# Head norms' root by bit operations on VectorE, projections placed behind the score matmuls, and the second page's request ahead of three low halves

## Chip, core and metric

The kernel runs on one core of one Trainium2 chip. The metric is the device time of one launch in microseconds (us), as the median of the runs; lower is better.

## What is computed

One layer of a decoder for a prompt of 1024 tokens and 32 sample tokens (8 sequences of 4). One input projection feeds two groups of heads: sparse attention (8 query heads, 2 key and value heads) over the keys that an indexer picks, and retention (8 heads) with a norm over each head. Both are gated, concatenated and projected out. Cut to what the change touches:

```python
def _index_select(qi, wi, ki, qpos, kpos, topk):
    s = jnp.einsum('bqhd,bsd->bqhs', qi, ki) * (D_IDX ** -0.5)
    score = jnp.einsum('bqh,bqhs->bqs', wi, jax.nn.relu(s))
    ...
    top_val, top_idx = lax.top_k(score, topk)      # 256 of the prompt's 1024; sample: of 8192 paged keys
...
def _head_norm(o):
    mu = jnp.mean(o, axis=-1, keepdims=True)
    var = jnp.mean(jnp.square(o - mu), axis=-1, keepdims=True)
    return (o - mu) * lax.rsqrt(var + EPS)
```

The outputs are y for prompt and sample, the new keys, values and indexer keys, and the retention's states.

## The kernel before

Tile's scheduler sets the order of each engine's instructions when the kernel is built; each engine then runs its list in that order. The program calls below say what belongs together, and the lists say what runs when. PE is TensorE, DVE VectorE, ACT ScalarE, POOL GpSimd and SP the queue that issues most transfers.

**Weights** (`load_w`, L176 on): a block of 256 columns is loaded as two halves of 512 rows on SP; ACT casts each half to the high part (`whi`, L196), and POOL subtracts to get the low part (`wlo`, L197) in eight pieces, one for each 128 rows. `wraw`, `whi` and `wlo` have two buffers each. A projection unit (`proj_b`, L277 to L279) is one block of 128 columns for one of three groups of tokens (384, 416 or 256), with 8 x 3 = 24 matmuls (high x high, low x high, high x low) into `pb`.

**Scores, up to some 166 us.** `index_scores` (L530 on) handles the query blocks qb 2 to 7 of 128 rows. For each of 8 indexer heads PE multiplies into one of two PSUM pairs `si` (L383, L384; (qb+1) x 128 columns), ACT takes the relu (L542, two buffers `r`) and DVE adds the weighted result to `score` (L543); at a block's end POOL masks the diagonal (L545). Between the heads, `unit(rate)` adds the rate to a counter and issues a projection unit of the generator `units` at each whole number: 12 units of qa (results copied to `qst` by ACT and DVE, L364, L365), 6 of keys and values (`kava`), 12 of the gate (`ga`). The rate is 0.3 in the blocks 5 to 7.

**Pages, up to some 297 us.** Sixteen pages of the sample's indexer keys follow (loop over b and a, L868 on). `key_pages` (L421) issues one indirect DMA from POOL's queue into a `slab`. The two slabs share the tag `big` with the two query tiles of the scores, so page 0's waits for the last matmul on `qis0`, page 1's for the last on `qis1`, and later ones for the `pox` matmuls of the page two before. DVE transposes each half (L875), PE multiplies (`pox`, L877), ACT takes a relu (`rl`, L880) and PE sums the heads (`py`). Between them go steps of the prompt's bisection for the 256th score (DVE, ACT; L700 to L733) and projection units, 2.5 a page at first, then 2.0 and 1.25.

**Retention, some 297 to 604 us.** Four pairs of heads hp 0 to 3. For each, `pqk` and `pvg` projections, rope on DVE (`rp`, L1116 to L1118), the chunked retention on PE (`ret`, `second`, masked by DVE as `sm`, L1148), and for hp 0 to 2 `norm_gate` (L1151 on), once for 128 rows x 16 and once for 32 rows x 2 numbers: statistics by DVE, `gv` = variance + eps (L1163), Sqrt on ACT (L1166, with a table load), reciprocal and one Newton step on DVE (L1167 to L1182), the scaling on ACT and DVE (L1186, L1188), the gate on POOL (L1191). The last pair's factors come from `last_factors` (L1200 on), which has the same root (L1209 to L1214). The selection of the sample's keys (`sel`, `cx`, `eq`) runs beside it on DVE. Attention follows (`sa`, L1743), then the output projection and the last gate.

## Time and profile before

| | |
|---|---|
| median of 3 runs | 1011.24 us (1006.64 to 1012.78) |
| profiled execution, own time | 1009.07 us |
| its span | 1007.0 us |
| mean granted clock of TensorE | 0.969 |
| busy: PE, DVE, ACT, POOL | 945.4, 664.2, 453.5, 338.8 us |

A row of a timeline reads: start, duration, engine, line, operation, out<-in, shapes, count, and in brackets the idle time ahead with what ended it. A row of windows gives for a stretch the busy time and count of each engine, the granted clock, the share of the DMA engines and GB/s. A row of waits reads: engine and line that waited, what it waited for, the total in us, how often, the longest.

### The profile page before, as it was taken

The page shows a single profiled execution, that of the slowest core. Times are in us where ns is not written, and L with a number is a line of the kernel's source. Part 1 is how long each engine was busy: PE and PEld are TensorE (multiplying, and loading weights), DVE is VectorE, ACT ScalarE, POOL GpSimd, SP SyncE. Part 2 cuts the span into 40 slices and gives each one's busy share as a digit, 9 for nine tenths or more (in the row PEclk, how much of TensorE's full clock was granted, in tenths as well). Part 3 has the DMA queues.
Part 4 walks back from the last instruction along what each step waited for, and adds up shares of the span by engine and source line. Part 5 has one row for each costly group of instructions (what it writes and reads, how often), then busy time and mean ns, then how long its engine had stood idle before and what let it go on. Part 6 is the DMA issues. An engine that isn't in the chain of part 4 may idle for free.

```text
span 1007.0 us, 18956 instructions
## 1 busy us (share of the span) xinstructions
PE 945.4 (94%) x6983; PEld 798.3 (79%) x6983; DVE 664.2 (66%) x1936; ACT 453.5 (45%) x1005; POOL 338.8 (34%) x444
## 2 busy tenths in 40 slices
PE   4999995989999999998899988999999999999998
PEld 3989993557678988988898866566567999999998
DVE  6747667879946669889679558777754323953332
ACT  5645555345324877224422537465554434432210
POOL 4205215112406326247325226454323322233300
PEclk8999998899999999999899968999999999999999
DMA  8323234567534112032013554533221312422211
GB/s 277 100 73 102 100 111 119 188 206 255 182 104 102 41 43 69 20 91 67 24 43 102 135 162 138 163 105 97 63 79 55 112 53 84 143 86 90 86 39 37
DMA packets 102127, 104.36 MB, mean 104 GB/s; under 512 B 22002, under 2 KB 92210, under 8 KB 99602
## 3 DMA queue, kind: packets, MB, share of 16 engines
q1 hardware_dynamic: 96274, 76.93, 25.8%
q0 software_dynamic: 5760, 26.22, 8.4%
q8 instruction: 55, 0.90, 0.4%
q14 instruction: 38, 0.31, 0.1%
HBM read 80.36 MB, written 22.76 MB: 102 GB/s over the span
## 4 chain that ended last, share of the span: by engine, by line
PE 63%; DVE 14%; DMA 9%; issue 8%; POOL 3%; ACT 2%; SPq 1%; DVEq 0%; POOLq 0%; ACTq 0%
PE pb L277 5%; PE pb L278 4%; PE pb L279 4%; PE ob L1772 3%; PE ptp L1764 3%; PE pg L287 3%; PE pg L289 3%; PE pg L288 3%; PE po L287 3%; PE po L288 3%; PE po L289 3%; PE pox L877 2%; DMA kx<-in_cache_kidx,kidx 2%; PE pvg L287 2%; PE pvg L288 2%
## 5 line engine op out<-in xcount | busy, mean ns | idle before, releaser
L1277 POOL DMA_INDIRECT kvs<-in_cache_kv,idx x64 | 64.2, 1004 | 59.0 <-ACT pT L1769 32.0
L287 PE MATMUL pvg<-whi_vgb,xh 128*128 128x256 f32 x256 | 77.0, 301 | 2.5 <-DVE rp L1118 2.5
L288 PE MATMUL pvg<-wlo_vgb,xh 128*128 128x256 f32 x256 | 75.8, 296 | 0.8 <-POOL wlo_vgb L197 0.8
L287 PE MATMUL pqk<-whi_qkb,xh 128*128 128x256 f32 x256 | 73.8, 288 | 1.5 <-DVE rp L1118 1.2
L289 PE MATMUL pvg<-whi_vgb,xl 128*128 128x256 f32 x256 | 74.6, 292 | 0.0
L287 PE MATMUL po<-whi_o,yTh 128*128 128x256 f32 x256 | 73.3, 286 | 0.4 <-DVE yaT L1783 0.4
L288 PE MATMUL pqk<-wlo_qkb,xh 128*128 128x256 f32 x256 | 73.3, 287 | 0.0
L289 PE MATMUL pqk<-whi_qkb,xl 128*128 128x256 f32 x256 | 73.1, 285 | 0.0
L288 PE MATMUL po<-wlo_o,yTh 128*128 128x256 f32 x256 | 72.9, 285 | 0.0
L287 PE MATMUL pg<-whi_g,yTh 128*128 128x256 f32 x256 | 72.7, 284 | 0.0
L289 PE MATMUL po<-whi_o,yTl 128*128 128x256 f32 x256 | 72.6, 284 | 0.0
L289 PE MATMUL pg<-whi_g,yTl 128*128 128x256 f32 x256 | 72.3, 282 | 0.0
L288 PE MATMUL pg<-wlo_g,yTh 128*128 128x256 f32 x256 | 72.2, 282 | 0.0
L197 POOL TENSOR_TENSOR wlo_g<-wraw_g,whi_g 128x256 fp32r<-128x256 f32 x32 | 27.1, 881 | 88.0 <-ACT whi_g L196 87.9
L1961 DVE TENSOR_TENSOR sgm<-pu,sgm 128x256 f32<-128x256 f32 x32 | 13.6, 424 | 64.5 <-PE pu L289 61.2
L1753 ACT ACTIVATE L<-L,mn 128x128 f32<-128x128 f32 (+7 forms) x64 | 49.6, 777 | 14.5 <-DVE mn L1749 14.1
L543 DVE SCALAR_TENSOR_TENSOR score<-r,wi,score 128x384 f32<-128x384 f32 (+5 forms) x42 | 42.6, 1015 | 20.2 <-ACT r L542 18.2
L287 PEld LDWEIGHTS pvg<-whi_vgb,xh 128*128 128x128 f32 x256 | 50.0, 195 | 4.6 <-issue 2.1
L288 PEld LDWEIGHTS pvg<-wlo_vgb,xh 128*128 128x128 f32 x256 | 50.0, 195 | 1.3 <-POOL wlo_vgb L197 1.0
L287 PEld LDWEIGHTS pqk<-whi_qkb,xh 128*128 128x128 f32 x256 | 48.3, 188 | 3.1 <-issue 2.4
L287 PEld LDWEIGHTS po<-whi_o,yTh 128*128 128x128 f32 x256 | 49.0, 191 | 2.2 <-issue 1.6
L289 PEld LDWEIGHTS pvg<-whi_vgb,xl 128*128 128x128 f32 x256 | 50.1, 196 | 0.3
(559 smaller groups left out, 3115.9 us busy)
## 6 DMA issues: line engine op xcount, KB each, us to landing
wraw_qkb<-in_w_in SPq DMA_DIRECT2D x16, 256.0 KB
wraw_vgb<-in_w_in SPq DMA_DIRECT2D x16, 256.0 KB
wraw_o<-in_w_out SPq DMA_DIRECT2D x8, 512.0 KB
qas<-qas_d SPq DMA_DIRECT2D x8, 512.0 KB
xr<-in_x_prompt SPq DMA_DIRECT2D x8, 512.0 KB
wraw_g<-in_w_ple_gate SPq DMA_DIRECT2D x8, 512.0 KB
out_y_prompt<-sgm SPq DMA_DIRECT2D x32, 128.0 KB
qas_d<-qst SPq DMA_DIRECT2D x8, 384.0 KB
```

Of the source, the lines that this page charges most:

```text
L197: nc.gpsimd.tensor_tensor(lo[:, k, :n], raw, hi[:, k, :n].bitcast(F32), op=ALU.subtract)
L277: nc.tensor.matmul(pt[:m, :n], wh, xh[:, k, ts], start=(k == 0), stop=False)
L278: nc.tensor.matmul(pt[:m, :n], wh, xl[:, k, ts], start=False, stop=False)
L279: nc.tensor.matmul(pt[:m, :n], wl, xh[:, k, ts], start=False, stop=(k == KC - 1))
L287: nc.tensor.matmul(pt[:, :n], ah, hi[:, k, :n], start=(k == 0), stop=False)
L288: nc.tensor.matmul(pt[:, :n], ah, lo[:, k, :n], start=False, stop=False)
L289: nc.tensor.matmul(pt[:, :n], al, hi[:, k, :n], start=False, stop=(k == kc - 1))
L543: nc.vector.scalar_tensor_tensor(sc, r[:, :n], wi[:, qb, h:h + 1], sc if h else place[:, :n], op0=ALU.mult, op1=ALU.add)
L1277: return nc.gpsimd.indirect_dma_start(out=dst, out_offset=None, in_=kvflat, in_offset=bass.IndirectOffsetOnAxis(ap=idx, axis=0))
L1753: behind[0] = nc.scalar.activation(L[:, :n], L[:, :n], AF.Exp, bias=least, scale=-1.0, accum_out=sm[:, i4:i4 + 1])
L1764: nc.tensor.transpose(tp[:, i4 * 128:i4 * 128 + 128], P[i4][:, kb * 128:kb * 128 + 128], ident)
L1772: nc.tensor.matmul(ob[64 * o:64 * o + 64, :256], vtok[:, kb, kv * 64:kv * 64 + 64], pT[:, o * 256:o * 256 + 256], start=(kb == 0), stop=(k ...
```

## The change

1. `inverse_root(y, z, v)`: eleven DVE operations (a shift, a subtraction from a constant on the bits, three Newton steps of three operations) in place of Sqrt, reciprocal and one Newton step, in `norm_gate` and in `last_factors`.
2. In the blocks 5 to 7, `between` counts 0.375 for each head instead of 0.3 and its units may be issued only behind a score matmul: the first three calls behind the last one of block 2, later ones behind the score matmul issued last. The units of the page loop stand behind the last score of all, at 2, 2.5, 2 and 2 for the first four pages and 12.5/12 after.
3. The low halves of `kava` are left at five; the other three are issued behind the request of page 1, which is now made ahead of the page loop.

```diff
@@ -173,7 +173,7 @@
 
     last_w = [None]
 
-    def load_w(name, pieces, lazy=False):
+    def load_w(name, pieces, lazy=False, late=0):
 
 
         n = sum(p[1] for p in pieces)
@@ -199,7 +199,12 @@
 
         if lazy:
             return hi, lo, raws, convert()
-        for _ in convert():
+        todo = convert()
+        for _ in range(KC - late):
+            next(todo)
+        if late:
+            return hi, lo, raws, todo
+        for _ in todo:
             pass
         return hi, lo, raws
 
@@ -377,11 +382,13 @@
             a = slice(o * 64, o * 64 + 64)
             nc.vector.tensor_tensor(kl[a, gs], s, kh[r0:r0 + 64, gs].bitcast(F32), op=ALU.subtract)
 
+    scored = [None, None]
+
     def mm_qk(pt, st, kh, kl, n):
         for c in range(0, n, 512):
             w = min(512, n - c)
             nc.tensor.matmul(pt[:, c:c + w], st, kh[:, c:c + w], start=True, stop=False)
-            nc.tensor.matmul(pt[:, c:c + w], st, kl[:, c:c + w], start=False, stop=True)
+            scored[1] = nc.tensor.matmul(pt[:, c:c + w], st, kl[:, c:c + w], start=False, stop=True).ins
 
     scp = ExitStack()
     sp_ = scp.enter_context(pool("scp"))
@@ -414,13 +421,15 @@
     def slab(name):
         return big.tile([128, 8, 384], F32R, tag="big", bufs=2, name=name)
 
+    paged = [None]
+
     def key_pages(i):
 
         b, a = i // 2, i % 2
         kx = slab("kx").bitcast(F32).rearrange("p a b -> p (a b)")
-        nc.gpsimd.indirect_dma_start(
+        paged[0] = nc.gpsimd.indirect_dma_start(
             out=kx[:, :2048], out_offset=None, in_=pages,
-            in_offset=bass.IndirectOffsetOnAxis(ap=kidx[:, a * 8 + b:a * 8 + b + 1], axis=0))
+            in_offset=bass.IndirectOffsetOnAxis(ap=kidx[:, a * 8 + b:a * 8 + b + 1], axis=0)).ins
         return kx
 
     def use_qa(j, g, pt):
@@ -487,7 +496,7 @@
                 proj_b(w, c0, 128, use, (g,))
                 yield
 
-        w = [load_w("qa0", wcols((QA, 256))), load_w("qa1", wcols((QA + 256, 256)))]
+        w.extend([load_w("qa0", wcols((QA, 256))), load_w("qa1", wcols((QA + 256, 256)))])
         loads = [("kava", KA), ("ga0", GA), ("ga1", GA + 256), None]
         for i in range(5):
             for a in range(2):
@@ -496,8 +505,9 @@
                        (lambda g, pt: use_ga(2 * i - 6 + a, g, pt)))
                 yield from triple(w[i], a * 128, use)
             if i < 3:
-                w.append(load_w(loads[i][0], wcols((loads[i][1], 256))))
-
+                w.append(load_w(loads[i][0], wcols((loads[i][1], 256)), late=0 if i else 3))
+
+    w = []
     unit_gen = units()
     tick = [0.0]
 
@@ -643,6 +653,7 @@
             nc.vector.tensor_scalar(place[:, i * 256:i * 256 + 256], C("slots"), i * 256.0, -1.0e-36,
                                     op0=ALU.add, op1=ALU.mult)
         index_scores(2, qiss[0])
+        scored[0] = scored[1]
         for qb in (3, 4):
             index_scores(qb, qiss[0], more)
         for _ in last:
@@ -651,8 +662,15 @@
         nc.sync.dma_start(O["kidx_sample"].rearrange("o b t d -> (o b t) d"), ktok[:NS, 8, :64])
         unit(0)
         kx0 = key_pages(0)
+        nth = [0]
+
+        def between():
+            nth[0] += 1
+            with tc.issue_after(scored[nth[0] > 3]):
+                unit(0.375)
+
         for qb in (5, 6, 7):
-            index_scores(qb, qiss[1], lambda: unit(0.3))
+            index_scores(qb, qiss[1], between)
 
     bss_ = ExitStack()
     bs = bss_.enter_context(pool("bs", side="right"))
@@ -865,10 +883,14 @@
         if pend:
             pend.pop(0)()
 
+    kxs = [kx0, key_pages(1)]
+    with tc.issue_after(paged[0]):
+        for _ in w[2][3]:
+            pass
     for b in range(8):
         rls = []
         for a in range(2):
-            kx = key_pages(2 * b + a) if b or a else kx0
+            kx = key_pages(2 * b + a) if b else kxs[a]
             po = pair("pox")
             for up in range(2):
                 kT = kx[:, 2048:] if up == 0 else sx.tile([128, 1024], F32, tag="kT", bufs=1, name="kT")
@@ -884,7 +906,8 @@
             while tickb[0] >= 1:
                 tickb[0] -= 1
                 step(bp)
-            unit(2.5 if 2 * b + a < 2 else 2.0 if 2 * b + a < 4 else 1.25)
+            with tc.issue_after(scored[1]):
+                unit((2, 2.5, 2, 2)[2 * b + a] if b < 2 else 12.5 / 12)
         pend.append(lambda b=b, rls=rls: head_sum(b, rls))
     while pend:
         later()
@@ -1148,6 +1171,16 @@
             nc.vector.tensor_tensor(sm[:rows, j, :rows], sc, mask_ap, op=ALU.mult)
         return r, qkT, sm
 
+    def inverse_root(y, z, v):
+
+        V = nc.vector
+        V.tensor_scalar(y.bitcast(I32), v.bitcast(I32), 1, None, op0=ALU.logical_shift_right)
+        V.tensor_scalar(y.bitcast(I32), y.bitcast(I32), -1.0, float(0x5F3759DF), op0=ALU.mult, op1=ALU.add)
+        for _ in range(3):
+            V.scalar_tensor_tensor(z, y, -0.5, y, op0=ALU.mult, op1=ALU.mult)
+            V.tensor_tensor(z, z, v, op=ALU.mult)
+            V.scalar_tensor_tensor(y, z, 1.5, y, op0=ALU.add, op1=ALU.mult)
+
     def norm_gate(acc, sgs, ntb, rows, tb0, hp):
 
         nh = ntb * 2
@@ -1163,23 +1196,8 @@
         nc.vector.tensor_tensor(v_.rearrange("p (t h) -> p t h", h=2),
                                 mv[:rows, :nh, 1].rearrange("p (t h) -> p t h", h=2),
                                 epsn[:rows, tb0:tb0 + ntb, 2 * hp:2 * hp + 2], op=ALU.add)
-        nc.scalar.activation(y_, v_, AF.Sqrt)
-        nc.vector.reciprocal(y_, y_)
-        one = [slice(i, i + 1) for i in range(nh)]
-        if nh == 2:
-            for i in one:
-                nc.vector.tensor_scalar(z_[:, i], y_[:, i], y_[:, i], v_[:, i], op0=ALU.mult, op1=ALU.mult)
-        else:
-            nc.vector.tensor_tensor(z_, y_, y_, op=ALU.mult)
-            nc.vector.tensor_tensor(z_, z_, v_, op=ALU.mult)
-        nc.vector.tensor_scalar(z_, z_, -0.5, 1.5, op0=ALU.mult, op1=ALU.add)
-        if nh == 2:
-            for n, i in enumerate(one):
-                nc.vector.tensor_scalar(y_[:, i], y_[:, i], z_[:, i], None, op0=ALU.mult)
-                nc.vector.tensor_scalar(z_[:, i], mv[:rows, n, 0:1], y_[:, i], -1.0, op0=ALU.mult, op1=ALU.mult)
-        else:
-            nc.vector.tensor_tensor(y_, y_, z_, op=ALU.mult)
-            nc.vector.scalar_tensor_tensor(z_, mv[:rows, :nh, 0], -1.0, y_, op0=ALU.mult, op1=ALU.mult)
+        inverse_root(y_, z_, v_)
+        nc.vector.scalar_tensor_tensor(z_, mv[:rows, :nh, 0], -1.0, y_, op0=ALU.mult, op1=ALU.mult)
         for i in range(nh):
             a = acc[:rows, i // 2, (i % 2) * 64:(i % 2) * 64 + 64]
             if i % 4 < 3:
@@ -1206,12 +1224,7 @@
         z = rt.tile([128, 18], F32, tag="gz", bufs=1, name="gz")
         nc.vector.tensor_tensor(v.rearrange("p (t h) -> p t h", h=2),
                                 lmv[:, :, 1].rearrange("p (t h) -> p t h", h=2), epsn[:, :, 6:8], op=ALU.add)
-        nc.scalar.activation(lrs, v, AF.Sqrt)
-        nc.vector.reciprocal(lrs, lrs)
-        nc.vector.tensor_tensor(z, lrs, lrs, op=ALU.mult)
-        nc.vector.tensor_tensor(z, z, v, op=ALU.mult)
-        nc.vector.tensor_scalar(z, z, -0.5, 1.5, op0=ALU.mult, op1=ALU.add)
-        nc.vector.tensor_tensor(lrs, lrs, z, op=ALU.mult)
+        inverse_root(lrs, z, v)
 
     smask = C("smask", 32)
     bmask = C("bmask")
```

What the scheduler makes of it stands in the lists. First PE, in the middle of the score stage; `si` are scores (`qis_349` the queries of blocks 2 to 4, `qis_771` those of 5 to 7), `pb` projections. Before, around the first head of block 5:

```order
L279 MATMUL pb<-xh,wlo_qa_1043 128x416
L383 MATMUL si<-kih,qis_349 128x512
L384 MATMUL si<-kil,qis_349 128x512
L383 MATMUL si<-kih,qis_349 128x128
L384 MATMUL si<-kil,qis_349 128x128
L277 MATMUL pb<-xh,whi_qa_1042 128x416
L383 MATMUL si<-kih,qis_771 128x512
L384 MATMUL si<-kil,qis_771 128x512
L383 MATMUL si<-kih,qis_771 128x256
L384 MATMUL si<-kil,qis_771 128x256
L278 MATMUL pb<-xl,whi_qa_1042 128x416
L279 MATMUL pb<-xh,wlo_qa_1043 128x416
```

Now, from the last head of block 4 over the first head of block 5, and then the last head ahead of the next projection:

```order
L390 MATMUL si<-kih,qis_349 128x512
L391 MATMUL si<-kil,qis_349 128x512
L390 MATMUL si<-kih,qis_349 128x128
L391 MATMUL si<-kil,qis_349 128x128
L390 MATMUL si<-kih,qis_771 128x512
L391 MATMUL si<-kil,qis_771 128x512
L390 MATMUL si<-kih,qis_771 128x256
L391 MATMUL si<-kil,qis_771 128x256
```

```order
L390 MATMUL si<-kih,qis_771 128x512
L391 MATMUL si<-kil,qis_771 128x512
L390 MATMUL si<-kih,qis_771 128x256
L391 MATMUL si<-kil,qis_771 128x256
L282 MATMUL pb<-xh,whi_qa_1034 128x416
L283 MATMUL pb<-xl,whi_qa_1034 128x416
```

From the second head of block 4 on, thirteen heads (7 of 640 columns, 6 of 768) stand together, where one or two stood between pieces of projection units before; behind them a whole unit stands after each two or three heads.

Second, the hand-over from the scores to the pages. PE before:

```order
L383 MATMUL si<-kih,qis_771 128x512
L384 MATMUL si<-kil,qis_771 128x512
L877 MATMUL pox<-kx,qbd 64x512 x2
L877 MATMUL pox<-kT,qbd 64x512 x2
L877 MATMUL pox<-kx,qbd 64x512 x2
L877 MATMUL pox<-kT,qbd 64x512 x2
L877 MATMUL pox<-kx,qbd 64x512 x2
L847 MATMUL py<-rl,wst 32x512
L850 MATMUL py<-rl,wst 32x512 x3
L277 MATMUL pb<-xh,whi_kava 128x384
```

PE now; the projection rows above the first `pox` are the last of the 24 rows of a unit, and those below it the first of the next:

```order
L390 MATMUL si<-kih,qis_771 128x512
L391 MATMUL si<-kil,qis_771 128x512
L282 MATMUL pb<-xh,whi_qa_1050 128x256
L283 MATMUL pb<-xl,whi_qa_1050 128x256
L284 MATMUL pb<-xh,wlo_qa_1051 128x256
L282 MATMUL pb<-xh,whi_qa_1050 128x256
```

```order
L283 MATMUL pb<-xl,whi_qa_1050 128x256
L284 MATMUL pb<-xh,wlo_qa_1051 128x256
L899 MATMUL pox<-kx,qbd 64x512 x2
L282 MATMUL pb<-xh,whi_qa_1050 128x384
L283 MATMUL pb<-xl,whi_qa_1050 128x384
L284 MATMUL pb<-xh,wlo_qa_1051 128x384
```

Before, the twelve units of qa are all ahead of the last score, and the pages' matmuls follow it at once. Now four of them (256, 384, 416 and 256 tokens) stand behind it, one ahead of the first `pox` and the others between the following ones. POOL before:

```order
L421 DMA kx<-in_cache_kidx,kidx 128x2048
L545 AFFINE_SELECT score<-score 128x128
L197 TENSOR_TENSOR wlo_kava<-wraw_kava_1432,whi_kava 128x256 x4
L197 TENSOR_TENSOR wlo_kava<-wraw_kava_1434,whi_kava 128x256 x4
L545 AFFINE_SELECT score<-score 128x128 x2
L197 TENSOR_TENSOR wlo_ga_1803<-wraw_ga_1804,whi_ga_1802 128x256 x4
L197 TENSOR_TENSOR wlo_ga_1803<-wraw_ga_1806,whi_ga_1802 128x256 x4
L421 DMA kx<-in_cache_kidx,kidx 128x2048
L545 AFFINE_SELECT score<-score 128x128
L421 DMA kx<-in_cache_kidx,kidx 128x2048 x3
```

POOL now:

```order
L430 DMA kx<-in_cache_kidx,kidx 128x2048
L555 AFFINE_SELECT score<-score 128x128 x3
L197 TENSOR_TENSOR wlo_kava<-wraw_kava_1392,whi_kava 128x256 x4
L197 TENSOR_TENSOR wlo_kava<-wraw_kava_1394,whi_kava 128x256
L430 DMA kx<-in_cache_kidx,kidx 128x2048
L197 TENSOR_TENSOR wlo_kava<-wraw_kava_1394,whi_kava 128x256 x3
L555 AFFINE_SELECT score<-score 128x128
L430 DMA kx<-in_cache_kidx,kidx 128x2048 x3
L197 TENSOR_TENSOR wlo_ga_1760<-wraw_ga_1761,whi_ga_1759 128x256 x4
L197 TENSOR_TENSOR wlo_ga_1760<-wraw_ga_1763,whi_ga_1759 128x256 x4
```

The request of page 1 (the second `kx`) stood behind sixteen low halves, eight of kava and eight of the first ga block. Now it stands behind five, and the eight of ga behind the requests of pages 2 to 4.

Third, DVE in the norm of the head pair hp 1. Before, from the root's next to last operations to the scaling:

```order
L1181 TENSOR_TENSOR gy<-gy,gz 128x16
L1163 TENSOR_TENSOR gv<-bmv,cst 32x2
L1116 TENSOR_TENSOR rp_7_5623<-pqk,cst 128x256
L1117 TENSOR_TENSOR rp_7_5624<-pqk,cst 128x4x32
L1118 TENSOR_TENSOR rp_7_5624<-pqk,cst 128x4x32
L1265 TENSOR_SCALAR sso<-sso,cst 128x512
L1338 SCALAR_TENSOR_TENSOR cx<-sel 128x1056
L1182 SCALAR_TENSOR_TENSOR gz<-bmv,gy 128x16
L1188 TENSOR_SCALAR acc_4539<-acc_4539,bmv,gy 128x64 x4
L1148 TENSOR_TENSOR sm<-ret,cst 128x128
```

Now, from the third Newton step to the scaling, and the 32-row root behind it:

```order
L1180 SCALAR_TENSOR_TENSOR gz<-gy 128x16
L1625 COPY sbd_2901<-ret 64x64 x2
L1171 TENSOR_TENSOR sm<-ret,cst 128x128
L1171 TENSOR_TENSOR sm<-second,cst 128x128
L1181 TENSOR_TENSOR gz<-gz,gv 128x16
L1182 SCALAR_TENSOR_TENSOR gy<-gz,gy 128x16
L1196 TENSOR_TENSOR gv<-bmv,cst 32x2
L1171 TENSOR_TENSOR sm<-ret,cst 128x128
L1200 SCALAR_TENSOR_TENSOR gz<-bmv,gy 128x16
L1206 TENSOR_SCALAR acc_4547<-acc_4547,bmv,gy 128x64 x4
L1623 TENSOR_TENSOR sbd_2900<-ret,sbd_2901 64x64 x2
L1171 TENSOR_TENSOR sm<-second,cst 128x128
```

`cx`, `eq` and `sel` are the selection's operations over 1056 or 2048 columns, `sm` the retention's masks. The steps of the 128-row root are spread between them in both lists, and there are five more of them now. The scaling stands ahead of the second `cx` before, and behind the last `eq` now.

## The prediction

> **What bounds the kernel now.** I read the page first, for the engine that sets the span.
>
> ```profile
> PE 945.4 (94%) x6983; PEld 798.3 (79%) x6983; DVE 664.2 (66%) x1936; ACT 453.5 (45%) x1005; POOL 338.8 (34%) x444
> ```
>
> PE is busy in 94% of the span of 1007 us, so the kernel can gain only where PE stands or runs at a low clock. The changed parts lie between 90 and 610 us; the table of windows shows which stretches there have room. The first figure behind the window is PE's busy time, and PEclk the granted clock.
>
> ```profile
> core 0: us, PE busy (x) PEld busy (x) DVE busy (x) ACT busy (x) POOL busy (x), PEclk, DMA share, GB/s
> 100.00:150.00 50.00, 49.76 (x296) 47.33 (x295) 32.35 (x45) 25.62 (x40) 10.46 (x12) 1.00 0.32 102
> 150.00:170.00 20.00, 13.28 (x67) 9.52 (x65) 16.93 (x17) 12.53 (x17) 12.86 (x11) 0.98 0.27 75
> 170.00:190.00 20.00, 13.60 (x53) 6.14 (x54) 14.72 (x39) 5.92 (x8) 3.03 (x4) 0.68 0.76 244
> 190.00:227.00 37.00, 34.38 (x189) 22.90 (x187) 30.39 (x84) 17.25 (x29) 6.80 (x10) 1.00 0.59 182
> 227.00:300.00 73.00, 73.00 (x431) 52.69 (x430) 55.47 (x110) 27.94 (x42) 19.88 (x31) 1.00 0.55 185
> 300.00:460.00 160.00, 154.94 (x1283) 141.61 (x1282) 124.98 (x410) 84.79 (x197) 68.21 (x114) 1.00 0.23 58
> 460.00:490.00 30.00, 23.68 (x167) 21.04 (x166) 29.42 (x65) 14.15 (x33) 22.62 (x27) 0.89 0.30 73
> ```
>
> From 100 to 227 us PE is idle for 0.24 + 6.72 + 6.40 + 2.62 = 16.0 us, nearly all of it right around the hand-over from scores to pages, and from 227 to 300 for nothing. The page stage therefore ends when PE's work ends, and whatever idle goes before it shortens the program. The view of waits names the longest things that PE stood for there, and one that will return:
>
> ```profile
> PE pox L877 <- DVE mv L713: 5.9, 1, 5.9
> PE pox L877 <- DVE kT L875: 4.2, 1, 4.2
> PE kvt L452 <- ACT kvs L448: 1.7, 1, 1.7
> ```
>
> The timelines of POOL, DVE and PE show why the two longest are there:
>
> ```profile
> 157.26 10.74 POOL L197 TENSOR_TENSOR wlo_ga<-wraw_ga,whi_ga 128x256 fp32r<-128x256 f32 x8 [4.33 <-ACT whi_ga L196]
> 168.15 1.75 POOL L421 DMA_INDIRECT kx<-in_cache_kidx,kidx  x1 [0.16 <-issue]
> ```
>
> ```profile
> 161.10 7.98 DVE L543 SCALAR_TENSOR_TENSOR score<-r,wi,score 128x1024 f32<-128x1024 f32 x5
> 176.98 1.25 DVE L875 STREAM_TRANSPOSE kx<-kx 128x1024 f32<-128x1024 f32 x1 [4.22 <-DMA kx<-in_cache_kidx,kidx]
> ```
>
> ```profile
> 165.23 1.08 PE L877 MATMUL pox<-kx,qbd 128*64 128x512 f32 x4 [0.46 <-ACT r L542]
> 170.48 1.98 PE L877 MATMUL pox<-kT,qbd 128*64 128x512 f32 x4 [4.17 <-DVE kT L875]
> 178.37 1.98 PE L877 MATMUL pox<-kx,qbd 128*64 128x512 f32 x4 [5.91 <-DVE mv L713]
> 180.10 1.95 PE L877 MATMUL pox<-kT,qbd 128*64 128x512 f32 x4
> 181.84 1.59 PE L877 MATMUL pox<-kx,qbd 128*64 128x512 f32 x4
> ```
>
> All qa projections are spent by then. PE issues the last score at about 164.8, DVE is still at its sums until 169.1, and page 1's request stands behind eight low halves until 168.15, though its slab was free with the last score. The data is usable at 176.98, 8.8 us behind the request. PE has nothing else, and behind that idle time the clock is halved: groups of four pox take 1.98, 1.98, 1.95 and 1.59 us instead of 1.08, which is 3.2 us more. So **16.0 + 3.2 = 19.2 us** is all that this stretch can give.
>
> **The projections kept back.** They are the same matmuls, so nothing is added to PE's work. What they give must be taken where they stood. Thirteen heads of scores (7 of 640 columns, 6 of 768) now run with no projection between. Two lines of DVE, a timeline row and a group by shape, and rows of PE price them:
>
> ```profile
> 98.93 1.88 DVE L543 SCALAR_TENSOR_TENSOR score<-r,wi,score 128x640 f32<-128x640 f32 x2 [1.85 <-ACT r L542]
> L543 DVE SCALAR_TENSOR_TENSOR score<-r,wi,score 128x768 f32<-128x768 f32 x4 | 4.0, 1008 | 0.1
> ```
>
> ```profile
> 105.85 0.34 PE L277 MATMUL pb<-xh,whi_qa 128*128 128x384 f32 x1
> 106.03 0.40 PE L383 MATMUL si<-kih,qis 128*128 128x512 f32 x1
> 106.66 0.39 PE L278 MATMUL pb<-xl,whi_qa 128*128 128x384 f32 x1
> 120.06 0.39 PE L383 MATMUL si<-kih,qis 128*128 128x512 f32 x1
> 120.76 0.39 PE L383 MATMUL si<-kih,qis 128*128 128x512 f32 x1
> ```
>
> DVE takes 0.94 us for a head of 640 and 1.01 plus a gap of some 0.06 for one of 768: 7 x 0.94 + 6 x 1.07 = 13.0 us. PE needs 0.63 and 0.70 from start to start: 8.6 us. The scores go through two PSUM pairs, so PE waits for the difference, **4.4 us**. The lower bound is 3.0, since two pairs let PE run two heads ahead (1.4 us); above it lie slow sums of 1.6 us a head, as the five at 161.10 while POOL subtracts (7.98 / 5), of which five more would cost 3. In the rest of the stage a whole unit follows each two or three heads. DVE falls behind by some 0.35 us a head, and a unit gives it 3 to 4.5 us, so PE sets the pace; I allow 0.5 us.
>
> Behind the last score now stand four qa units of 24 matmuls. One of 384 columns takes 0.18 us from start to start (105.85 to 106.03), 4.2 us a unit; by their columns those of 256 and 416 take 2.8 and 4.5, and the four 14.3. Page 1 is asked for at the last score: only five low halves (5 x 1.34 = 6.7 us) precede it on POOL, and their casts stand on ACT ahead of the last eight heads. With the 8.8 us above it is usable before PE has done three of the units, 11.5 us. Page 2 needs page 0's slab, which is released by pox about 8 us in, so it comes 16.8 us in, and PE gets there at 14 to 15: a wait of about 2 us. Page 4 waits in the same way for some 1.5 us, and the kvt for 0.5 to 1.7, as it does now. Together **4 us** (2 to 9) instead of what stands there now. DVE gets the four units' copies behind the scores instead of before, an estimated 6 us; it is busy 14.7 + 30.4 + 55.5 = 100.6 of the 130 us from 170 to 300, so it can take them. The three halves of kava that run behind the request, 3 x 1.34 = 4 us, come 14 us before their projection: nothing. The eight of the next weights now stand behind page 4's request and ahead of page 5's; that can make page 5 late by up to 5 us, half hidden by two kava units, and it is in the upper bound.
>
> Gain of this part: 19.2 - 4.4 - 0.5 - 4.0 = **10.3 us**, between 19.2 - 7.4 - 0.5 - 9 = 2.3 and 19.2 - 3.0 - 2.0 = 14.2.
>
> **The root.** Six calls in the heads lose a Sqrt, and its table on ACT, and gain DVE operations. An added DVE operation is dear only where DVE is full, which 460 to 490 is (29.42 of 30).
>
> ```profile
> 479.72 1.28 ACT L1166 ACT_TABLE_LOAD   x1
> 481.01 0.20 ACT L1166 ACTIVATE gy<-gv 32x2 f32<-32x2 f32 x1
> ```
>
> ```profile
> 469.26 0.16 DVE L1181 TENSOR_TENSOR gy<-gy,gz 128x16 f32<-128x16 f32 x1
> 473.18 0.36 DVE L1182 SCALAR_TENSOR_TENSOR gz<-bmv,gy 128x16 f32<-128x16 f32 x1
> ```
>
> ACT loses eleven loads of 1.28 and seven roots of 0.2, 15.5 us with that of the last head, but it is busy 84.79 of 160 us from 300 to 460 and 14.15 of the next 30, so it is no bound. DVE gets some 36 operations of 0.15 to 0.2 us more, 6 us over 250 us, about 1 of it in the full stretch. Against this stands the hop to ACT, some 1.5 us with its load (479.72 to 481.21), in each of six calls. Most of both is hidden behind PE, so I take **1 us of gain**, between 6 lost (every added operation on PE's path) and 6.3 won (all of PE's idle time in the full stretch).
>
> In the last head the root lies on PE's path:
>
> ```profile
> 602.10 0.18 DVE L1207 TENSOR_TENSOR gv<-wi,cst 128x18 f32<-128x18 f32 x1
> 602.57 0.27 DVE L1210 RECIPROCAL wi<-wi 128x18 f32<-128x18 f32 x1 [0.28 <-ACT wi L1209]
> 602.87 0.18 DVE L1211 TENSOR_TENSOR gz<-wi 128x18 f32<-128x18 f32 x1
> 603.08 0.18 DVE L1212 TENSOR_TENSOR gz<-gz,gv 128x18 f32<-128x18 f32 x1
> 603.82 0.29 DVE L1749 CUSTOM_DVE_ANT_0 L<-sa,near 128x128 f32<-128x128 f32 x1
> 604.17 0.47 PE L1743 MATMUL sa<-kahi,qas 128*128 128x128 f32 x1 [2.55 <-DVE mn L1749]
> ```
>
> From gv's end at 602.28 to 603.82 are 1.54 us now. Eleven dependent operations, 0.21 us from start to start as 602.87 to 603.08, make 2.4: **0.9 us lost**.
>
> **Sum.** 1009.07 us is the profiled execution's own time: 1009.07 - 10.3 - 1.0 + 0.9 = 998.7. The median of the runs, 1011.24, lies 2.2 above it; beside that median I expect 1000.
>
> **The rivals.** First, the hand-over keeps its waits: the ring of two slabs paces the first pages, so PE spends the four units and then waits for pages 2 to 6 about 2 us each, 10 instead of 4, and 3 more for slow sums. That gives 1006 to 1009, within 1%. For it speaks that a page takes 8.8 us from request to use; against it, that from 227 on, at the same depth, PE never waits.
>
> Second, **slower**: the eleven dependent operations are strung out on a full DVE. The chain has 4 us between two of its steps, 469.26 and 473.18, since selection's large operations stand between them in the order; with five more steps, acc comes back up to three qk units later in the first head pair, and the next retention starts as late. Where PE has no projections left then, it stands as in 460 to 490: 6.3 us idle and 0.11 x 30 = 3.3 of clock, 9.6 together. One more such stretch cancels the gain; at two, in two pairs of heads, it is 1000 + 19.2 = 1019. It decides from the point where acc is later than the last projection of its pair. For it speaks DVE's 29.42 of 30; against it, that from 300 to 460, with two such calls in it, PE still lost only 5.1 of 160 us.
>
> Third, the clock falls in the thirteen heads, where PE is busy some 8.6 of 13 us in pieces. At half clock a head takes PE 1.26 or 1.40 us, 17.2 in all, 4.2 more than DVE: 1004. Between 150 and 170 PE is busy 13.28 of 20, with 0.98 granted, so I give it little. [...]
>
> Fourth, the full stretch of 460 to 490 meets PE's projections better and most of its 9.6 us goes: about 991. That the change does not do what it says is excluded for the order, which shows the thirteen heads and the four units.
>
> **Chances.** Forecast 0.50 (its own range 994 to 1006), hand-over 0.20, slower 0.13, clock 0.07, fourth 0.10. About 1% is what a measurement of this kernel tells from no change: below 1001.1 lie the fourth and 0.35 of the forecast, 0.45; above 1021 would be needed for slower, and the second rival with what else may go wrong passes it at most with 0.10; the rest, 0.45, is within 1%. The range that leaves 2 in 10 out is 989 to 1012.
>
> **What would show it.** Right: the waits of 4.17 and 5.91 us are gone, pox groups stand at about 1.08 us, page 1's request comes within 1 us of the last score, at about 152, and the first pqk starts at 285 to 290 instead of 297; si waits for r by 4 to 5 us between 94 and 108; sa waits some 3.4 us instead of 2.55. Wrong: pqk starts later than 294 (first rival), more idle than 9 us for sm, rp or ret between 330 and 560 (second), or a granted clock of 0.5 between 95 and 110 (third).

## The result and the profile after the change

The change made the kernel slower: 1018.59 us (median of 7 runs, 1015.01 to 1026.66) against 1006.64 us before (7 runs, 1005.88 to 1012.78), a ratio of 1.011 with a 95% interval of 1.007 to 1.015. Forecast were 1000 us and a range up to 1012. The profiled execution of the change took 1015.01 us, its fastest, 5.9 us above that of before; so the profile shows about half of what the medians do. The profile of x4 below, whose lists in the retention are those of the change and which took 1020.15 us, shows more of it.

The page of the changed kernel, span and busy times:

```profile
span 1013.2 us, 18991 instructions
PE 947.4 (94%) x6983; PEld 800.8 (79%) x6983; DVE 665.6 (66%) x1972; ACT 435.0 (43%) x987; POOL 330.8 (33%) x444
```

PE does the same 6983 matmuls; ACT has lost 18.5 us of work and DVE gained 36 instructions. Where the time went shows if both kernels are cut at the same milestones: last score, first `pqk`, first `sa`, first `po`. Before, then after, the two stretches between last score and first `sa`, and the one behind:

```profile
164.80:297.50 132.70, 119.56 (x648) 80.01 (x652) 104.74 (x232) 52.18 (x80) 34.25 (x44) 0.95 0.58 189
297.50:600.10 302.60, 286.34 (x2325) 258.94 (x2317) 229.52 (x780) 139.86 (x349) 123.93 (x195) 0.96 0.29 76
```

```profile
153.70:294.10 140.40, 131.59 (x744) 94.54 (x746) 109.11 (x244) 56.94 (x91) 40.03 (x53) 0.99 0.62 197
294.10:604.80 310.70, 286.67 (x2325) 258.64 (x2317) 230.80 (x810) 123.08 (x333) 121.89 (x195) 0.97 0.28 73
604.80:777.20 172.40, 165.38 (x1232) 106.68 (x1229) 120.03 (x451) 95.31 (x219) 70.66 (x74) 0.95 0.33 97
```

The columns are start and end, length, then busy time and instructions of PE, PE's loads, DVE, ACT and POOL, the granted clock, DMA share and GB/s. The last score comes at 153.7 instead of 164.8, and the first `pqk` at 294.1 instead of 297.5: of 11.1 us ahead, 3.4 are left. The retention stretch takes 310.7 us instead of 302.6, with the same PE work (286.7 and 286.3 us), so nearly all of the 8.1 us are PE standing idle (24.0 us against 16.3). In x4's profile the same stretch took 314.8 us, with 22.1 idle and a granted clock of 0.94:

```profile
295.90:610.70 314.80, 292.74 (x2324) 263.98 (x2316) 232.43 (x810) 123.21 (x333) 122.17 (x195) 0.94 0.28 73
```

So one profile places such a stretch only to some 4 us. Attention takes 172.4 instead of 169.5 (before: 600.1 to 769.6).

At the hand-over the long waits are gone, as forecast, and the request comes 0.2 us behind the last score:

```profile
153.94 2.00 POOL L430 DMA_INDIRECT kx<-in_cache_kidx,kidx  x1 [13.03 <-PE si L391]
```

```profile
PE kvt L461 <- ACT kvs L457: 3.9, 3, 3.4
PE si L390 <- ACT r L552: 3.0, 7, 1.3
PE pox L899 <- DVE kT L897: 2.2, 2, 1.7
PE pox L899 <- DVE kx L897: 1.6, 1, 1.6
PE py L865 <- DVE qst L370: 0.9, 1, 0.9
```

In their place stands a wait that was called a small one, `kvt` for ACT's copy `kvs`, which itself waits for a transfer (ACT's timeline):

```profile
207.52 0.37 ACT L457 COPY kvs<-pb 128x256 f32<-128x256 f32 x1 [6.10 <-DMA out_k_prompt<-kvs]
```

In the retention the root of hp 1, 128 rows, reads on DVE's timeline (some of its eleven steps, the variance first, the scaling's factor last):

```profile
468.63 0.42 DVE L1196 TENSOR_TENSOR gv<-bmv,cst 128x16 f32<-128x16 f32 x1
470.23 2.35 DVE L1351 TENSOR_TENSOR_SCAN cx<-sel 128x1056 f32<-128x1056 bf16 x1
472.50 0.37 DVE L1177 TENSOR_SCALAR gy<-gv 128x16 int32<-128x16 int32 x1
...
477.16 0.37 DVE L1178 TENSOR_SCALAR gy<-gy 128x16 int32<-128x16 int32 x1
...
482.40 0.16 DVE L1180 SCALAR_TENSOR_TENSOR gz<-gy 128x16 f32<-128x16 f32 x1
...
494.27 0.17 DVE L1200 SCALAR_TENSOR_TENSOR gz<-bmv,gy 128x16 f32<-128x16 f32 x1
```

That is 25.6 us from variance to factor for eleven steps that work some 2.2 us; before, it was 17.2, from the row below to the one at 473.18 in the prediction.

```profile
455.96 0.17 DVE L1163 TENSOR_TENSOR gv<-bmv,cst 128x16 f32<-128x16 f32 x1
```

Over the three pairs the way from variance to factor is 20.6 + 25.6 + 18.7 = 65 us against 6.2 + 17.2 + 14.5 = 38. One that waits for it shows in ACT's waits, before and after (ACT copies the next pair's results into `acc`, which has one buffer):

```profile
ACT acc L1618 <- DMA yb_d<-acc: 3.0, 2, 2.3
```

```profile
ACT acc L1631 <- DMA yb_d<-acc: 7.7, 2, 5.6
```

In the last pair the root stands on PE's path as forecast:

```profile
606.82 0.18 DVE L1225 TENSOR_TENSOR gv<-wi,cst 128x18 f32<-128x18 f32 x1
609.47 0.29 DVE L1762 CUSTOM_DVE_ANT_0 L<-sa,near 128x128 f32<-128x128 f32 x1
```

From 607.00 to 609.47 are 2.47 us (forecast 2.4, before 1.54), and `sa` waits 3.5 us (2.55 before).

### The profile page after: what moved, and what is told of

Read it like the earlier page. It is cut to its first block, busy times and chain, and to the rows that moved or that the text cites. A ratio compares the mean times of both kernels' runs of the same rounds, so it can differ in the third digit from the quotient of the medians.

```text
span 1013.2 us, 18991 instructions
## 1 busy us (share of the span) xinstructions
PE 947.4 (94%) x6983; PEld 800.8 (79%) x6983; DVE 665.6 (66%) x1972; ACT 435.0 (43%) x987; POOL 330.8 (33%) x444
## 4 chain that ended last, share of the span: by engine, by line
PE 63%; DVE 17%; DMA 8%; issue 5%; ACT 4%; SPq 1%; POOL 1%; ACTq 0%; DVEq 0%; POOLq 0%
PE pb L282 4%; PE pb L284 4%; PE pb L283 4%; PE ob L1785 4%; PE ptp L1777 3%; PE pg L292 3%; PE pg L294 3%; PE pg L293 3%; PE po L292 3%; PE po L293 3%; PE po L294 3%; PE pvg L292 2%; PE pvg L294 2%; PE pvg L293 2%; PE sa L1756 2%
## 5 line engine op out<-in xcount | busy, mean ns | idle before, releaser
L292 PEld LDWEIGHTS pg<-whi_g,yTh 128*128 128x128 f32 x256 | 48.7, 190 | 1.6 <-issue 1.6
```

The lines of the kernel that those rows point to most:

```text
L292: nc.tensor.matmul(pt[:, :n], ah, hi[:, k, :n], start=(k == 0), stop=False)
```

## The experiments

Each ratio is to the kernel before, run on the same chip, with its 95% interval. "Stretch" is first `pqk` to first `sa` in the profile: 302.6 us before, 310.7 with the change. The runs were made in four groups, and the kernel before had its own median in each: 1007.10 us (x1 to x4), 1011.21 (x5 to x8), 1014.42 (x9 to x12) and 1007.26 (x13, x14). Ratios of different groups are therefore compared with care.

A new norm also makes the scheduler write other lists. PE's order in the stretch is that of the kernel before in x1, x8, x10, x11 and x13, and that of the change in x4. In the change, x2, x5 and x6 it leaves that of the kernel before at some 390 us, and in x9 it leaves that of the change at some 415 us. So what such a version gains or loses includes its new order; no run changes the norm and keeps the order.

**x1, the old root in the changed kernel** (`norm_gate` and `last_factors` as before).

> The change without its root: Sqrt on ACT, reciprocal and one Newton step stand again in norm_gate and last_factors; the projections and the page's request stay as changed. Theory A (the eleven dependent operations, strung out on a full DVE, cost the retention stage its 7 us): from the first pqk to the first sa it takes about 302 to 304 us as before the change, and since the first pqk comes some 2.5 us earlier the time is 0.993 to 0.999 of the kernel before. Theory B (projections moved ahead let selection and retention meet badly, whatever the root): it stays near 309 us, and the ratio near 1.007 to 1.01. Page stage in both: first pqk near 295.

Ratio 0.9989 (0.9967 to 1.0012); first `pqk` 293.9, stretch 301.0. Theory A holds, and the projections' part alone is worth nothing that can be measured.

```profile
293.90:594.90 301.00, 283.58 (x2324) 257.47 (x2316) 229.20 (x780) 139.74 (x349) 123.94 (x195) 0.97 0.29 76
```

**x2, the new root in the kernel before.**

> The kernel before with the new root alone. Theory A: first pqk at 297 as before, from there to the first sa 308 to 312 us, ratio 1.006 to 1.012. Theory B: within 0.3% of the kernel before, the stretch at 302 to 305 us. If both causes are needed together: both this and the old root in the changed kernel are at 1.000 or below.

Ratio 1.0154 (1.0132 to 1.0176), stretch 314.0: more than theory A gave, and no less than the whole change (the intervals overlap). The root alone is enough for the loss.

```profile
297.60:611.60 314.00, 291.62 (x2325) 261.68 (x2317) 232.05 (x810) 123.11 (x333) 122.47 (x195) 0.96 0.28 73
```

**x3, the estimate by bits alone.**

```diff
-        for _ in range(3):
+        for _ in range(0):
```

> The changed kernel with the three Newton steps left out, so that the root is the first estimate by bits alone: a chain of two DVE operations in place of eleven, nothing on ACT. Theory A: the stretch from the first pqk to the first sa falls below that before the change, to 298 to 302 us, sa waits for DVE about 1 us less than with eleven, and the ratio is 0.985 to 0.997. Theory B: the stretch stays at 307 us or more.

Ratio 0.9985 (0.9953 to 1.0017), stretch 300.6; variance to factor 9.3 us over three pairs. The cost is gone, though the ratio lies just above the range of theory A: a chain a quarter as long as the old one gains nothing beside it (x1), so with 38 us the factor seems to be in time already.

**x4, the third part undone** (`late=0`, page 1's request in the loop).

> The changed kernel with its third part undone: all eight low halves of the key and value weights ahead of the second page's request, and the request back in the page loop. In the profile of the change, these halves ended 13 us ahead of the request, so the theory is that their three add 3 us there and delay nothing: first pqk within 1 us of 295, ratio to the kernel before within 0.3% of the full change's 1.011. Rival: the request's place in the loop costs the first pages some 3 us, first pqk at 298.

Ratio 1.012 (1.0087 to 1.0154); first `pqk` 295.9, as the theory has it. The time is that of the full change: this part does nothing that can be measured.

**x5, more work on DVE without a longer chain** (in the kernel before, behind each norm's store).

```diff
+        gx = rt.tile([128, 16], F32, tag="gx", bufs=1, name="gx")
+        for _ in range(8):
+            nc.vector.tensor_scalar(gx[:rows, :nh], mv[:rows, :nh, 1], 2.0, None, op0=ALU.mult)
```

> The kernel before, old root, with eight small DVE operations more for each of the six head norms (48 in all, where the change has 36), which write a scratch tile that nothing reads and on which no scaling waits. Theory (the root costs because its dependent steps come back late, 37.9 us from the variance to the factor over three pairs before the change and 65 after, and hold the one buffer acc): the factor comes at most 3 us later a pair, and the ratio to the kernel before is 0.998 to 1.005. Rival (the root costs by the work that it adds to a full DVE): the ratio is 1.01 or more, and the stretch from the first pqk to the first sa grows by 8 us or more.

Ratio 1.0112 (1.0068 to 1.0156), stretch 307.5, variance to factor 44.3 us. By its time the rival holds too: with 48 small operations more, the kernel is about 1% slower, though the chain grew little. The profile does not show DVE as the cause.

```profile
295.80:603.30 307.50, 290.45 (x2325) 262.54 (x2317) 234.51 (x828) 142.02 (x351) 123.77 (x195) 0.95 0.29 75
```

Of the 4.9 us in the stretch (8 or more were expected) only 0.8 are PE standing idle (307.50 less 290.45 is 17.1, against 16.3 before); the other 4.1 are the same 2325 matmuls busy for longer (290.45 us against 286.34), at a granted clock of 0.95 against 0.96. Another 6.5 lie in attention (176.0 us), where the granted clock was 0.95 against 0.97 before. Why the clock was lower is not settled.

**x6, a long chain without work on DVE** (in the kernel before).

```diff
         nc.scalar.activation(y_, v_, AF.Sqrt)
+        for _ in range(16):
+            nc.scalar.copy(y_, y_)
```

> The kernel before, old root, with sixteen dependent copies of the root's result in place on ACT ahead of the reciprocal: a chain as long as the new root's, but nothing added to DVE, and on an engine that is half idle there. Theory (late factor, one acc): variance to factor grows from 38 to 55 us or more over the three pairs, and the ratio is 1.006 to 1.016. Rival (DVE's work): 0.998 to 1.004, since DVE gets nothing.

Ratio 1.0101 (1.0059 to 1.0142), stretch 310.4, variance to factor 21.2 + 20.0 + 13.3 = 54.6 us, just short of the 55 expected; DVE is busy 229.1 us in the stretch, as before, and PE idle 23.3 (310.40 less 287.07) against 16.3, at the same granted clock (0.96). So a late factor, with the order that the scheduler then makes, costs without any work added to DVE.

```profile
296.50:606.90 310.40, 287.07 (x2325) 258.87 (x2317) 229.12 (x780) 158.02 (x447) 125.45 (x195) 0.96 0.29 74
```

**x7, five Newton steps** (`range(5)`).

> The changed kernel with five Newton steps in place of three: a chain of seventeen operations. Theory (late factor): variance to factor grows from 65 to 85 us or more, the stretch from the first pqk to the first sa from 310.7 to 316 to 325, ratio to the kernel before 1.016 to 1.03; sa waits some 1.3 us longer. Rival (the step from seven to eleven passes a threshold and nothing more is lost behind it): ratio as in the change, 1.009 to 1.014.

Ratio 1.0172 (1.0135 to 1.0209), stretch 317.2, variance to factor 79 us, less than expected since six more steps brought 14 us. That speaks against a threshold behind which more steps are free, but does not exclude it: the interval overlaps a little with that of the change, and PE's idle time in the stretch is the same (317.20 less 293.04 is 24.2, against 24.0), with a granted clock of 0.94 against 0.97.

```profile
293.40:610.60 317.20, 293.04 (x2325) 264.61 (x2317) 236.60 (x846) 123.94 (x333) 125.58 (x195) 0.94 0.28 72
```

**x8, flatter rates, old root.**

```diff
-                unit((2, 2.5, 2, 2)[2 * b + a] if b < 2 else 12.5 / 12)
+                unit((2, 2, 1.5, 1.5)[2 * b + a] if b < 2 else 1.25)
```

> The changed kernel with the old root, and with the projection units spread more evenly over the pages: 2, 2, 1.5, 1.5 for the first four and 1.25 after, in place of 2, 2.5, 2, 2 and 12.5/12. Theory for the page stage (units of keys and values follow each other so closely that their staging tile waits for its transfer out, 3.4 us at 208 in the change): PE's wait of kvt for ACT falls below 2 us, first pqk comes at 290 to 293 instead of 294, ratio 0.993 to 0.999. Rival: the wait only moves, to page transposes, and first pqk stays at 294 or later.

Ratio 0.9953 (0.9918 to 0.9987), but first `pqk` 296.1 and a `kvt` wait of 5.1 us: the theory of spacing fails in the profile, and the ratio's interval overlaps that of x1.

**x9, acc in three tiles, the full change otherwise** (blocks 0 to 3, 4 to 7 and the sample's, each gated, stored and released by itself).

```diff
-        acc = rt.tile([128, 9, 128], F32, tag="acc", bufs=1, name=f"acc{hp}")
+        wholes = [rt.tile([128, n, 128], F32, tag=f"acc{i}", bufs=1, name=f"acc{i}_{hp}") for i, n in enumerate((4, 4, 1))]
+        acc = [wholes[t // 4][:, t % 4] for t in range(9)]
...
-        nc.sync.dma_start(yb_d[:rows, tb0:tb0 + ntb, hp, :], acc[:rows, :ntb, :])
+            if t % 4 == 3 or ntb == 1:
+                t0 = t // 4 * 4
+                nc.sync.dma_start(yb_d[:rows, tb0 + t0:tb0 + t + 1, hp, :], wholes[t0 // 4][:rows])
```

> The full change, new root and all, with the retention's result acc split into three tiles (blocks 0 to 3, 4 to 7, and the sample's), each stored and released by itself; the root's steps keep their places between the projections. Theory (the late factor costs because it holds the one acc): the copies into acc wait for the store of the pair before less than 4 us instead of 7.7, the stretch from the first pqk to the first sa falls from 310.7 to 303 to 308, ratio to the kernel before 1.001 to 1.009. Rival (only DVE's added work costs): the stretch stays at 309 to 314 and the ratio at 1.009 to 1.015.

Ratio 1.0004 (0.9972 to 1.0036), stretch 307.8, with a chain nearly as long as in the change (21.2 + 23.0 + 15.2 = 59 us).

```profile
ACT acc L1634 <- DMA yb_d<-acc: 3.2, 1, 3.2
```

By ratios the same root costs 1% less when half of `acc` can be refilled while the other half is still being stored, and ACT waits 3.2 us for it instead of 7.7. In this group x10 has the old root at 0.9992, so here hardly anything of the root's cost is left. This supports that the late factor costs through what it holds, but does not show it: the unsplit change was not run in this group (its median elsewhere, 1018.59, is 0.3% above the 1015.96 here), the order changed too, and the profile shows only 2.9 us of the gain in the stretch; it was one of the slower of the ten executions (1018.19 us).

**x10, no stores of the prompt's keys and values, old root.**

> The changed kernel with the old root and without the stores of the prompt's new keys and values (two outputs are not written), so that their staging tiles come free without a transfer. Theory for the page stage (it gives back 4 to 5 us since staging tiles wait for transfers out in a stage whose DMA engines are busy to two thirds): PE's wait of kvt for ACT falls from 4 us to 2 or less and the first pqk comes at 289 to 292 instead of 294. Rival (that wait stands beside others of the same length): first pqk at 293 or later.

Ratio 0.9992 (0.997 to 1.0013), first `pqk` 297.8: the rival holds. The wait moved (`kvt` 3.5, a gate projection 3.4), and the first copy of `kvs` still waited 7.1 us, for a store of qa.

**x11, two units kept instead of four, old root.**

```diff
-                unit(0.375)
+                unit(0.45)
...
-                unit((2, 2.5, 2, 2)[2 * b + a] if b < 2 else 12.5 / 12)
+                unit((2, 2, 1.5, 1.5)[2 * b + a] if b < 2 else 1.25)
```

> The changed kernel with the old root and two projection units behind the last score instead of four (0.45 a head, then 2, 2, 1.5, 1.5 and 1.25 a page). Theory: the run of heads without a projection shrinks to twelve, the pages' first waits stay covered, and less of the key and value stage collides with transfers: first pqk 290 to 294, ratio 0.992 to 0.998. Rival (two units do not cover page 1's 8.8 us): PE waits 3 us or more there and the ratio is 0.998 to 1.003.

Ratio 0.9913 (0.9886 to 0.9939): with x12 the lowest here, and below the theory's range. Beside x10 of the same group, which has four units kept, the median is 0.6% lower (1006.95 and 1013.52). First `pqk` is 293.9 in this profile.

**x12, the same with acc in three tiles.**

> The run above (old root, two units kept) with acc in three tiles as well. Theory (acc's release also holds the old root's pairs, 3.0 us in the kernel before): 1 to 4 us less than the run above, ratio 0.988 to 0.996. Rival (with the short chain acc is free in time): the same as the run above within 0.2%.

Ratio 0.9928 (0.99 to 0.9956), the same as x11: with the short chain `acc` is free in time. Up to the first `pqk` PE, DVE, ACT and POOL have the lists of x11, and in x14 too, yet it comes at 286.6 here and 287.8 there, within the 285 to 290 that were forecast for the change. In the row from the last score on, PE is idle for 5.6 us (128.80 less 123.24):

```profile
157.80:286.60 128.80, 123.24 (x693) 87.13 (x696) 106.27 (x239) 56.39 (x86) 40.78 (x57) 1.00 0.64 210
```

**x13, the kept units not stored, old root, four units.**

> The changed kernel with the old root, and without the stores of the four projection units that stand behind the last score (attention reads the first two groups of heads twice instead). Theory for the page stage (the four units bring their stores into a stage with busy DMA engines, and the staging tiles that the key and value units need next come free only with them): kvt's wait for ACT falls from 4 us to 2 or less, the copy of the first kvs no longer waits 7 us for a transfer, first pqk at 288 to 292. Rival (DVE's and the pages' own order sets the pace): first pqk at 293 to 298 as in the other runs with four units kept.

Ratio 0.9959 (0.9933 to 0.9985), first `pqk` 288.9, PE idle from the last score on for 2.8 us (in the last row below, 135.70 less 132.87) instead of 7.3 in x1 and 8.8 in the change, and a `kvt` wait of 2.4 us, a little more than the theory gave. The first of ACT's copies of `kvs`, in x1 and here, and the stretch from the last score to the first `pqk`:

```profile
189.33 0.48 ACT L457 COPY kvs<-pb 128x384 f32<-128x384 f32 x1 [7.02 <-DMA qas_d<-qst]
```

```profile
182.17 0.48 ACT L458 COPY kvs<-pb 128x384 f32<-128x384 f32 x1 [2.24 <-DVE kst L476]
```

```profile
153.20:288.90 135.70, 132.87 (x740) 95.12 (x743) 109.28 (x244) 57.20 (x91) 40.82 (x53) 0.99 0.60 194
```

The kept units' stores hold the two staging tiles that the key and value units need next (`qst`, `kvs` and `kst` share one tag with two buffers). In this version the scheduler also moved some groups of `pox` and `kvt` by a few places on PE, so a part of the 5.0 us against x1 can be the order.

**x14, the new root with two units kept and acc in three tiles.**

> The new root with acc in three tiles and two projection units behind the last score: the version with the best page stage and the root of the change. Theory (with acc released by parts the chain costs little, and what is left is DVE's added work): 0.992 to 1.000, and 0.2 to 0.8% above the run with the old root, two units and acc in three tiles. Rival (the root is then free, or gains by the table loads it saves): equal to that run or below, 0.987 to 0.993.

Ratio 1.0014 (0.9985 to 1.0043), stretch 310.1 against 304.1 in x12: with `acc` split, the new root still costs something against the old one, which x9 beside x10 did not show. How much is open: the ratios of the two groups lie 0.9% apart (the theory gave 0.2 to 0.8), the medians 0.2% (1008.40 and 1006.21), the stretches 6.0 us.

## Why the prediction was wrong

**The root is the step that failed.** It was taken as 1 us of gain, with the words "Most of both is hidden behind PE". Measured are 8.1 us lost in the stretch of the change and 11.4 in x2, and x1, which takes only the root back, loses nothing. The bound of 6 lost counted the added operations at their own durations (36 of some 0.17 us), as if a step took what it works. On a full DVE (29.6 of the 30 us from 460 to 490 here) a step takes what stands ahead of it in the order: 25.6 us for eleven. The 4 us between two steps were quoted for the slower rival and not used in the sum, and neither `acc`'s one buffer nor its store was in it.

**The second rival came nearest, and only in part.** That its time, 1019, is what came (1018.59) is luck: it stood on a kernel before of 1011.24, and the one beside the result took 1006.64, so 8 us were forecast by it and 12 lost. What it named as its condition, `acc` coming back late, is supported by x6, where a longer chain alone costs, and by x9. Its own sign does not tell: more than 9 us of idle for `sm`, `rp` or `ret` between 330 and 560 were to set it apart, and PE's waits of these kinds add up to 9.2 in the change, but to 9.1 before too. Of the 7.7 us of added idle only 2.9 lie between 330 and 560; 3.7 lie behind, up to the first `sa`, where a `ret` waits 1.9 us for ACT's copy into `acc`. Its argument against itself, that PE lost only 5.1 of 160 us from 300 to 460 "with two such calls in it", looked at the old chain, whose factor was still in time. And it had no place for added work on DVE, with which x5 is 1.1% slower. Chain (x6) and work (x5) each cost about 1%, and x2, which has both, 1.5%. Whether the two overlap, these intervals do not say, and which part of the root's cost is lateness, which is work and which is the new order stays open.

**The hand-over was mis-sized by its end.** Its first half held: thirteen heads, last score at 153.7 (about 152 forecast), no wait of 4.17 or 5.91, `pox` at 1.08, page 1 asked for at once. Of 19.2 us to be had, the term of 4.4 for the scores measured 5.5: from the first head (93.09) to the projection behind the thirteenth (107.20) are 14.1 us, less the 8.6 of PE. As waits of `si` for `r` only 1.1 us of it show between 94 and 108, not 4 to 5, since a matmul's row lasts beyond the start of the next: the one at 93.09 lasts 0.50 us, and the next begins at 93.43. The term of 4.0 for new waits measured 8.8, and with 3 us at half clock (granted 0.50 from 209 to 212, 0.78 over 210 to 215) the gain was 3.4, not 10.3. In the eight profiles with four units kept and stored, first `pqk` lies between 293.4 and 298.0, and in the four with the old scores between 295.8 and 297.6, so the usual gain is rather 1 to 2 us. That is the size of the first rival, whose sign (first `pqk` later than 294) came too, but not its cause: all waits of `pox` for DVE's transposes are 3.8 us, and `kvt` alone has 3.9. What was left out: the four units were costed as matmuls, with their DVE copies, and not with their stores. With them two transfers of 384 KB and two of 256 went into a stage in which the 16 DMA engines are busy to 0.62, through two staging tiles. Without them x13's first `pqk` comes 8.6 us ahead of the kernel before, close to the 10.3.

**The last factors** were right: 0.9 us forecast, 2.47 - 1.54 = 0.93 measured (eleven steps of 0.21 us make 2.3 rather than 2.4).

**The third rival** did come, and cost nothing that shows: the granted clock fell to 0.50 in the thirteen heads (97 to 99, last section), and from the first score matmul to the last are 98.3 us in the change (55.0 to 153.3) and 98.1 in x9 (55.8 to 153.9), whose first 154.3 us ran at 1.00. The fourth, that the select stretch improves, did not come: from 460 to 490 PE is idle 5.4 us instead of 6.3, at a granted clock of 0.86 instead of 0.89.

## What to carry to other kernels

A dependent chain on a full engine (DVE here, 29.58 of the 30 us from 460 to 490) is to be priced by the distance of its steps in the order, read from the profile, and then by what its result holds: here one buffer, whose release the next retention waits for. Replacing a hop to a half-idle engine (ACT, busy 14.15 of those 30 us before) by eleven steps on the fullest one lost 1.5% (x2); lateness alone (x6) and added operations alone (x5) each lose about 1%. And work moved to fill a hole brings its stores along: count the transfers and the staging tiles of the stage that it is moved into; two units filled the hole here better than four, and that version (with the old root) is 0.9% below the kernel before of its group.

## What the runs showed of the hardware

In the thirteen heads PE stood idle for no more than 0.50 us at a time, and still the granted clock fell; two rows of PE and the window of the change:

```profile
94.49 0.50 PE L390 MATMUL si<-kih,qis 128*128 128x512 f32 x1 [0.50 <-ACT r L552]
95.86 0.53 PE L390 MATMUL si<-kih,qis 128*128 128x512 f32 x1 [0.46 <-ACT r L552]
```

```profile
95.00:100.00 5.00, 4.54 (x17) 3.77 (x17) 4.62 (x7) 3.08 (x5) 0.97 (x2) 0.66 0.40 146
```

PE shows as busy 4.54 of 5 us there, but a matmul's row lasts beyond the start of the next (0.50 us at 94.49, the next at 94.83): by starts, the heads ahead of the fall come 1.40 and 1.37 us apart (93.09, 94.49, 95.86), and PE needs some 0.63 us for each. By slices of 1 us it was granted 1.00 from 95 to 96, 0.60, 0.50 and 0.50 up to 99, and 0.70 up to 100. What made it fall is not shown: x9, with the same thirteen heads, ran at 1.00 up to 154.3 us, with no `si` row above 0.51 us, where the row at 98.21 of the change lasts 0.75.

The tail of the last pair ran at half clock before (granted 0.52 from 585 to 605, 0.50 up to 609) and at 1.00 in the change (585 to 604.8), where attention's first 17 us then had half clock (0.50 from 604.8 to 622.0, PE busy 13.20 us). By an estimate from these rows, PE's 13.20 us there would be some 6.6 at 1.00, so this moved several us between the two stretches. In the other runs attention varies as well: it took 169 to 178 us in the profiles (169.5 at 0.97 before, 177.6 at 0.94 in x11), with the same matmuls (1230 to 1232 rows).
